# Head work paced by an account of every operation and transfer, loads recorded a step ahead, and q^T S of the samples as fp32 products with a masked q

## The chip, the cores and the metric

The kernel runs on one core of a Trainium2 chip. The metric is the device time of one execution in microseconds (us). TensorE (PE) multiplies, VectorE (DVE) and ScalarE (ACT) do elementwise work, GpSimd (POOL) does small elementwise work and issues transfers, SyncE (SP) issues transfers only. Each engine takes its instructions in the order in which they were recorded.

## The reference

One inference step of a one-layer recurrent decoder on a prompt of 512 tokens and on 8 samples of one token each, 520 columns in all. One projection of x (2048 wide) feeds three mixers: A has 8 heads of 128, B and C have 4 heads of 256. Then come the branch projections, weighted by sigmoid gates, the output projection and a LayerNorm. Cut to what the change touches:

```python
    (hq, hf, hi, hz, rq, rk, rv, rz, mq, mk, mv, mz, mo, mi, mf, gates) = jnp.split(x @ w_in, SPLIT_POINTS, axis=-1)
    ...
    def step(s, inp):                      # mixer A, one chunk of the sequence
        qc, kc, vc, gc = inp
        bc = jnp.cumsum(gc, axis=1)
        o = jnp.einsum('bthk,bhkv->bthv', qc * jnp.exp(bc), s)
        ...
        s_new = jnp.exp(last)[..., None] * s + jnp.einsum('bshk,bshv->bhkv', k_dec, vc)
    ...
    branch = jnp.einsum('blnc,ncd->blnd', ys, w_br)
    merged = jnp.sum(jax.nn.sigmoid(gates.reshape(bsz, seq_len, N_BRANCH, D_MODEL)) * branch, axis=2)
    out = merged @ w_o
```

For a sample a head has a state S of its own (128 x 128 in A, 256 x 256 in B and C). It is decayed, gets k v^T added, is written back, and the head's output is q^T S.

## The kernel before

**Dense work.** Every large product runs as two TensorE products in a rounded fp32 type: a weight tile w is split into `hi` (ACT writes it) and `lo` = w - hi (DVE writes it), and hi goes against both parts of x, lo against the upper one. The program is a list of items. An item is 24 or 48 matmuls of 260 columns on one split of 1024 columns. `w_in` is done in 76 units of 256 columns: 2 classical ones, then 74 by Strassen's scheme with 7 items each, whose sums of weight blocks DVE forms in the ring tiles `R` (three of 1 MB) or a DMA forms in `TT` (a second load that accumulates). Then follow 24 branch units and 8 output units. In all this makes 16,656 dense matmuls, `PD<-...` in the profile. Items share three buffers `hi`, two buffers `lo` and four PSUM banks `PD`.

Results of the projection are parked in DRAM (`pk_Af`, `pk_rv`, ...). Gates (`pk_g`) and partial sums (`pk_part`) come back in the branch units, where DVE multiplies them with the banks (L1542, L1546, `bfin`).

**Side work.** The heads run beside the dense items, as Python generators in three queues: preparation, prompt heads (`a_head`, `b_head`, `c_head`) and samples (`a_samp`, `bc_samp`). The dense generator yields every six matmuls, and then `side_step` may let each queue record its next step. Twelve slots `SL` of 520 columns hold what the heads load and compute; `room` and `ssl` share them out. Four more serve the dense work.

**What sets the order.** Nothing is scheduled by a compiler: what is recorded first stands first on its engine. When the next step of a queue is recorded, a small account decides (`Clock`, `TICK`): it adds up estimated TensorE time, and DVE and ACT time on top of it, without operands and without transfers. A step that yields d is due again d x 0.72 us of accounted TensorE time later; `yield 7` after a load is the whole provision for its landing. A step whose operands are late makes its engine wait, and all recorded behind it on this engine waits too.

`dense` records `lo` of the next item, the loads of weights and `hi` of the item after next at the start of an item:

```python
            if i + 1 < len(items):
                items[i + 1].lo()
            it.run("pre")
            for n in nxt.get(i, ()):
                loads[n]()
            if i + 2 < len(items):
                items[i + 2].hi()
```

The q^T S of a sample is formed in `a_samp` and `bc_samp` by scaling the rows of S with q (ACT, DVE), splitting the result with `hilo` (`qsh` by ACT, `qsl` by DVE) and multiplying both with a column of a unit matrix (`e8`) that puts the sum over the rows into the sample's row of one PSUM tile `os`.

Lines: L80 stands for all operations of TensorE, DVE and ACT, since one helper records them; L381 loads weights, L469 and L470 load `TT`, L654 loads parked tiles, L1136 and L1141 load a sample's state and its v (`vs`).

Of the kernel before, what the change touches and what calls it, by code (L numbers as in the profile page):

```python
# [39 lines left out]
class Clock:  # L40

    def __init__(self):
        self.pe = self.dve = self.act = 0.0

    def add(self, eng, us):
        if eng == "pe":
            self.pe += us
        else:
            setattr(self, eng, max(getattr(self, eng), self.pe) + us)


class Counted:
# [3 lines left out]
    def __getattr__(self, op):  # L56
        f = getattr(self._e, op)
        if op in ("dma_start", "preload_act_table_set"):
            return f

        def g(*a, **kw):
            out = kw.get("out", a[0] if a else None)
            big = out
            if op in ("tensor_reduce", "bn_stats"):
                big = kw["in_"]
            n = 1
            for s in big.shape[1:]:
                n *= s
            if self._n == "pe":
                if op == "transpose":  # L70
                    c = 0.109
# [3 lines left out]
            elif self._n == "dve":  # L75
                c = (n + 65) / 960.0
            else:
                c = 0.1 + 0.00085 * n
            self._c.add(self._n, c)
            return f(*a, **kw)  # L80
        return g


TICK = 0.72
# [4 lines left out]
def tile_hybrid_step(  # L89
# [16 lines left out]
    G, SY = nc.gpsimd, nc.sync  # L106
# [51 lines left out]
    held = {"scan": 0, "samp": 0}  # L158

    def sl(who="scan"):  # L160
        t = free["h"].popleft()
# [5 lines left out]
    def ssl():  # L167

        while not spare():
# [3 lines left out]
    def spare(n=1):  # L173
        return len(free["h"]) - n >= max(0, scan_need[0] - held["scan"])

    scan_need = [SCANMAX]

    def room(n):

        scan_need[0] = n  # L180
        while len(free["h"]) < n - held["scan"]:
            yield 1

    def dsl():
        n = 0
        while not free["d"]:
            n += 1
# [10 lines left out]

    def ps():
        return pss.tile([128, 512], F32, tag="s", name="s")  # L200

    def po1():
        return pso.tile([128, 512], F32, tag="os", name="os")
# [22 lines left out]
    e8 = const.tile([128, 8, 8], F32R, name="e8")  # L226
# [35 lines left out]
    class Side:  # L262
# [8 lines left out]
        def step(self):  # L271
# [15 lines left out]
    SLD, SLA = 2.0, 2.0  # L287

    def side_step(force=False):
        for q in (prepq, scanq, sampq):  # L290
            if force or (q.due <= clk.pe and clk.dve - clk.pe <= SLD and clk.act - clk.pe <= SLA):
# [26 lines left out]
    class Item:  # L318

        def __init__(self, src, mm, post=None, keep=None, nosplit=False):  # L320
            self.src, self.mm, self.post, self.hooks = src, mm, post, {}
            self.n = len(items)
            self.keep, self.nosplit = keep, nosplit
            items.append(self)
# [58 lines left out]
    def strassen_unit(col, deint, fin):  # L383
# [11 lines left out]
        def prod(xn, bank, start, stop):  # L395
            xa, xb = X(xn, 0), X(xn, 1)

            def mm(it):
# [7 lines left out]
                for i, (w, x) in enumerate(seq):  # L406
                    T.matmul(o, w, x, start=start and i == 0, stop=i == 23, skip_group_check=not start)
                    if i % 6 == 5 and i < 23:
                        yield
# [55 lines left out]

        if prev and not deint:
# [3 lines left out]
            before.hook(3, lambda: G.dma_start(out=TT, in_=blk(1), accum_op=ADD))  # L470
# [3 lines left out]
        if prev:  # L474
            prev["P4"]()
# [129 lines left out]
    def dense():  # L605
# [7 lines left out]
        for i, it in enumerate(items):  # L613
            it.run("first")
            if i + 1 < len(items):
# [8 lines left out]
            for _ in it.mm(it):  # L624
                yield
                k += 1
                it.run(k)
# [24 lines left out]
    def ld(nm, k):  # L652
        s = sl()
        SY.dma_start(out=v3(s[:, 0:S], 2), in_=d2(ptile(f"{nm}{k}"))[:, :, 0:256])  # L654
# [23 lines left out]
    def hilo(t):  # L678
        hh = small.tile([128, 256], F32R, tag="qsh", name="qsh", bufs=1)
# [1289 lines left out]
```

## Time and profile before

| | us |
|---|---|
| median of 3 runs (2508.32 to 2512.08) | 2510.2 |
| the profiled execution's own time | 2511.26 |
| its span, first to last instruction | 2509.5 |
| TensorE busy | 2318.8 |
| VectorE busy | 1658.9 |
| ScalarE busy | 1102.3 |
| mean granted TensorE clock | 0.969 |

TensorE is the busiest engine. A busy TensorE is not one at its full pace: matmuls overlap, so the pace is read from the starts of rows that follow each other. Where a group's line names a releaser, this is what ended the engine's idle time before it. In the timeline a row merges equal instructions that follow each other. An fp32 product of TensorE stands in the trace as two records (72 products of 256 columns in the program are 144 records), one in the rounded type as one. From 0 to 190 us the kernel starts up, from 190 to 430 heads hardly take part, from 430 to 1230 the heads of A and B and from 1230 to 1975 those of C and most samples run beside the projection; the branch units reach to 2278 and the output units to the end.

### The profile page before, as it was taken

How to read it: one execution, taken by the hardware profiler on the slowest of the kernel's cores; microseconds unless marked ns; L12 is line 12 of the kernel's file. 1: busy time of each engine (PE TensorE's matmuls, PEld its weight loads, DVE VectorE, ACT ScalarE, POOL GpSimd, SP SyncE). 2: the span in 40 equal slices, each digit the busy share in tenths (PEclk: the TensorE clock that was granted, in tenths of full speed). 3: DMA queues.
4: the chain of work that ended last, by engine and by line, in shares of the span. 5: the costliest groups of instructions: out<-in, count | busy, mean ns of one | idle time of the engine just before them, and what ended most of it. 6: DMA issues, size and time to landing. Idle time of an engine off the chain costs nothing.

```text
span 2509.5 us, 45478 instructions
## 1 busy us (share of the span) xinstructions
PE 2318.8 (92%) x18525; PEld 2265.9 (90%) x18525; DVE 1658.9 (66%) x2648; ACT 1102.3 (44%) x1834; POOL 483.7 (19%) x654
## 2 busy tenths in 40 slices
PE   6999999999998999989889999999989999899995
PEld 6899999999998899989789899898989999899995
DVE  4877777787776767777567676777667444453336
ACT  4444444455544444545455555555546321222222
POOL 1032221223221221212122121221222000001002
PEclk9999999999998999999899999999999999999998
DMA  5376665556555565756567787888878657745221
GB/s 169 93 176 190 173 171 166 154 173 178 162 168 158 160 189 177 235 167 190 147 206 203 202 239 203 209 209 228 219 189 225 190 201 240 266 146 177 80 85 68
DMA packets 406769, 450.30 MB, mean 179 GB/s; under 512 B 17024, under 2 KB 358944, under 8 KB 405024
## 3 DMA queue, kind: packets, MB, share of 16 engines
q1 hardware_dynamic: 314992, 313.43, 39.6%
q0 software_dynamic: 91424, 133.90, 22.5%
q8 instruction: 145, 2.38, 0.4%
q14 instruction: 64, 0.52, 0.1%
q10 hardware_dynamic: 144, 0.07, 0.0%
HBM read 364.03 MB, written 83.28 MB: 178 GB/s over the span
## 4 chain that ended last, share of the span: by engine, by line
PE 35%; DMA 11%; DVE 7%; ACT 2%; issue 2%; SPq 1%; POOL 0%; DVEq 0%; ACTq 0%; POOLq 0%
PE PD L80 31%; DMA R<-in_w_in_dram 4%; PE s L80 3%; DMA SL<-pk_g 3%; DVE SL L80 2%; DVE lo L80 2%; DVE R L80 1%; ACT hi L80 1%; DMA SL<-pk_mv 1%; DMA SL<-pk_mo 1%; PE os L80 1%; DMA SL<-pk_mk 1%; DMA TT<-in_w_in_dram 1%; DMA SL<-vs 0%; DMA R<-in_w_branch_dram 0%
## 5 line engine op out<-in xcount | busy, mean ns | idle before, releaser
L80 PE MATMUL PD<-XZ,hi 128*128 128x260 f32 x9888 | 1443.6, 288 | 49.9 <-ACT hi L80 21.2
L80 PEld LDWEIGHTS PD<-XZ,hi 128*128 128x128 f32 x9888 | 1301.4, 192 | 60.7 <-ACT hi L80 24.5
L80 ACT ACTIVATE hi<-R 128x1024 fp32r<-128x1024 f32 (+1 forms) x539 | 566.6, 1058 | 691.3 <-PE PD L80 264.9
L80 DVE TENSOR_TENSOR lo<-R,hi 128x1024 fp32r<-128x1024 f32 (+1 forms) x538 | 646.7, 1204 | 286.2 <-PE PD L80 110.5
L80 PE MATMUL PD<-XZ,lo 128*128 128x260 f32 x4928 | 806.0, 287 | 12.4 <-DVE lo L80 12.4
L80 PEld LDWEIGHTS PD<-XZ,lo 128*128 128x128 f32 x4928 | 685.9, 191 | 14.7 <-DVE lo L80 14.1
L80 ACT ACTIVATE SL<-PD 128x260 f32<-128x260 f32 x304 | 114.5, 378 | 244.5 <-PE PD L80 164.0
L80 DVE TENSOR_TENSOR R<-R,R 128x1024 f32<-128x1024 f32 x148 | 180.3, 1218 | 14.5 <-DMA R<-in_w_in_dram 14.5
L646 POOL COPY smp<-SL 128x8 f32<-128x8 f32 x104 | 77.0, 740 | 546.9 <-ACT SL L80 322.5
L80 PE MATMUL s<-SL 128*128 128x64 f32 (+5 forms) x976 | 168.0, 311 | 13.9 <-ACT SL L80 7.2
L80 DVE TENSOR_TENSOR SL<-PD,SL 128x260 f32<-128x260 f32 x222 | 94.4, 425 | 126.6 <-PE PD L80 93.3
L80 DVE TENSOR_TENSOR SL<-SL 128x256 f32<-128x256 f32 (+9 forms) x315 | 146.6, 502 | 41.9 <-PE s L80 20.5
L80 PE MATMUL PD<-X,hi 128*128 128x260 f32 x1184 | 159.0, 285 | 0.0
L80 PEld LDWEIGHTS s<-SL 128*128 128x128 f32 (+1 forms) x976 | 139.3, 193 | 21.4 <-ACT SL L80 7.8
L470 POOL DMA_DIRECT2D TT<-in_w_in_dram x57 | 91.4, 1604 | 347.5 <-DMA TT<-in_w_in_dram 300.4
L80 PEld LDWEIGHTS PD<-X,hi 128*128 128x128 f32 x1184 | 149.3, 190 | 0.5
L80 ACT ACTIVATE SL<-SL 128x512 f32<-128x512 f32 (+5 forms) x160 | 88.3, 567 | 60.2 <-DVE SL L80 50.7
L637 POOL TENSOR_TENSOR rstd<-rva,half 128x4 f32<-128x4 f32 (+3 forms) x35 | 52.0, 1485 | 319.8 <-DVE rva L80 318.9
L80 PE MATMUL s<-ident,SL 128*128 128x128 f32 x389 | 68.1, 295 | 46.1 <-DMA SL<-pk_rv 16.0
L80 PEld LDWEIGHTS s<-ident,SL 128*128 128x128 f32 x389 | 49.4, 150 | 52.2 <-issue 26.7
L80 DVE TENSOR_TENSOR SL<-SL,PD 128x260 f32<-128x260 f32 x96 | 36.5, 422 | 88.9 <-DMA SL<-pk_g 58.4
L80 DVE TENSOR_TENSOR lo<-TT,hi 128x1024 fp32r<-128x1024 f32 x74 | 90.0, 1217 | 3.2 <-ACT hi L80 3.2
(221 smaller groups left out, 1610.1 us busy)
## 6 DMA issues: line engine op xcount, KB each, us to landing
R<-in_w_in_dram SPq DMA_DIRECT2D x150, 1024.0 KB, 6.1
TT<-in_w_in_dram SPq DMA_DIRECT2D x57, 512.0 KB, 6.3
TT<-in_w_in_dram POOLq DMA_DIRECT2D x57, 512.0 KB, 6.3
R<-in_w_branch_dram SPq DMA_DIRECT2D x24, 1024.0 KB, 5.7
out_dram<-SL POOLq DMA_DIRECT2D x88, 256.0 KB, 5.7
R<-in_w_out_dram SPq DMA_DIRECT2D x16, 1024.0 KB, 5.7
pk_g<-SL POOLq DMA_DIRECT2D x48, 260.0 KB, 4.6
SL<-pk_g SPq DMA_DIRECT2D x48, 260.0 KB, 6.0
```

What stands on the lines that cost most here:

```text
L80: return f(*a, **kw)
L470: before.hook(3, lambda: G.dma_start(out=TT, in_=blk(1), accum_op=ADD))
L637: G.tensor_tensor(out=r[0:p, 0:n], in0=a[0:p, 0:n], in1=half[0:p, 0:n], op=ALU.pow)
L646: G.tensor_copy(d2(sm(nm, k)), d2(o)[:, :, 256:HN])
```

## The change

1. **The account.** `Clock` keeps a time for each engine, POOL and SP included, the time at which each slot, tile or piece of `XZ` was last written and read, and one pipe for transfers. An operation starts when its engine and its operands are ready. `Side.step` makes the next step due 0.2 us after the latest operation or awaited transfer of this one (and 0.3 us of TensorE time later at the earliest); the number after `yield` no longer counts. Loads marked `pre=True` are not awaited there; instead `late(...)` keeps a head stepping idly until the account has them landed. fp32 products are charged 0.00085 us a column, half of before.
2. **Loads a step ahead.** In A the next head's f and q are loaded during this head, v and z together; in B k with q, in C q and k with v; z before the norm; in the branch units gates and partial sums are asked for one unit earlier, into a head's slot if need be.
3. **Dense order.** `dense` yields every three matmuls. The weight loads and `hi` of the item after next are recorded after 12 matmuls of an item instead of at its start, the first item of a Strassen unit (`late`) gets hi at the start of the item before it and lo after 12 matmuls, and the accumulating load of `TT` is issued 18 matmuls later.
4. **q^T S.** `qmask` multiplies q with the unit matrix into `qmt` (128 x 8 x 8, one column of q in its own row), and TensorE multiplies its slices with S itself in fp32. The scaling of S by q, `hilo` and their 96 + 96 operations are gone. In B and C the update of S is recorded in two halves of 256 columns instead of one of 512, the second in place of v.

```diff
+    def op(self, eng, cost, outs, ins):
+        t = self.t[eng]
...
+        for k in ki:
+            t = max(t, self.after(self.w, k, eng))
+        for k in ko:
+            t = max(t, self.after(self.w, k, eng), self.after(self.r, k, eng))
+        self.t[eng] = e = t + cost
...
+        self.pipe = max(self.pipe, t) + n / (300e3 if n > 4e5 else 230e3)
+        end = max(self.pipe, t) + (3.0 if accum else 2.0)
...
-                    c = max(0.06, 0.00046 * n) if a[2].dtype == F32R else 2 * max(0.06, 0.00085 * n)
+                    t = max(0.06, 0.00046 * n) if a[2].dtype == F32R else max(0.06, 0.00085 * n)
...
-TICK = 0.72
+TICK = 0.3
...
-                    d = next(self.q[0][1])
-
-                    self.due = max(clk.pe + (d or 1) * TICK, clk.dve + 0.5, clk.act + 0.5)
+                    clk.latest = 0.0
+                    next(self.q[0][1])
+
+                    self.due = max(clk.pe + TICK, clk.latest + 0.2)
...
+    def late(*ts):
+        return not forced[0] and clk.ready(*ts) > clk.pe + 0.5
...
-            if force or (q.due <= clk.pe and clk.dve - clk.pe <= SLD and clk.act - clk.pe <= SLA):
+            if force or (q.due <= clk.pe and clk.dve <= clk.next + SLD and clk.act <= clk.next + SLA):
...
+            clk.next = clk.pe + 2.87
+            if i + 1 < len(items) and not items[i + 1].late:
                 items[i + 1].lo()
             it.run("pre")
-            for n in nxt.get(i, ()):
-                loads[n]()
-            if i + 2 < len(items):
-                items[i + 2].hi()
+            if i + 1 < len(items) and items[i + 1].late:
+                items[i + 1].hi()
...
+                if k == 2:
+                    for n in nxt.get(i, ()):
+                        loads[n]()
+                    if i + 1 < len(items) and items[i + 1].late:
+                        items[i + 1].lo()
+                    if i + 2 < len(items) and not items[i + 2].late:
+                        items[i + 2].hi()
...
+    def qmask(q, e):
+
+        t = qmt[:, e]
+        V.tensor_tensor(out=t, in0=e8, in1=q.unsqueeze(2).to_broadcast([128, NS, 8]), op=MUL)
+        return t
...
+        if h < 7 and f"Af{h + 1}" in done and f"Aq{h + 1}" in done:
+            ahead[h + 1] = ld("Af", h + 1, True), ld("Aq", h + 1, True)
...
                 for b in bs:
                     st = lds.pop(b)
-                    V.scalar_tensor_tensor(out=tm[b][:, 0:256], in0=st[:, 256:512], scalar=q[1][:, b:b + 1],
-                                           in1=tm[b][:, 0:256], op0=MUL, op1=ADD)
+                    for e in range(2):
+                        T.matmul(po[0:NS, 0:256], qm[e][:, b, :], st[:, e * 256:(e + 1) * 256],
+                                 start=(b == 0 and e == 0), stop=(b == 7 and e == 1))
                     fr(st)
                 yield 1
-                for b in bs:
-                    hh, ll = yield from hilo(tm[b][:, 0:256])
-                    fr(tm[b])
-                    yield 1
-                    T.matmul(po[0:NS, 0:256], e8[:, b, :], hh, start=(b == 0), stop=False)
-                    T.matmul(po[0:NS, 0:256], e8[:, b, :], ll, start=False, stop=(b == 7))
...
         v = [ld("mv", 2 * h), ld("mv", 2 * h + 1)]
-        yield 7
+        q = [ld("mq", 2 * h + e, True) for e in range(2)]
+        k = [ld("mk", 2 * h + e, True) for e in range(2)]
+        yield 1
...
         for t in range(2):
-            items[k + t].hook(1, sigload(n, 2 * i + t))
+            if (n, i) != (0, 0):
+                items[k - 2 + t].hook(2, sigload(n, 2 * i + t, False))
+            items[k + t].hook(1, sigload(n, 2 * i + t, True))
```

How far a load is ahead of its reader can be counted in the recorded program: the dense matmuls recorded between the load (SP or POOL) and the first instruction that reads its slot, median over the loads of a kind.

| load | before | after |
|---|---|---|
| `pk_rv` (B, v) | 42 | 87 |
| `pk_mv` (C, v) | 45 | 100 |
| `pk_mk` (C, k) | 48 | 229 |
| `pk_mo` (C, output gate) | 48 | 73 |
| `pk_Af` (A, f) | 54 | 99 |
| `vs` (samples, v) | 42 | 84 |
| `pk_g` (branch gates) | 54 | 132 |
| `R` from `in_w_in` | 48 | 60 |

The same count from `hi` to the first product that reads it is 48 before in 519 items; after, it is 36 in 445 items and 24 in 73. From `lo` it is 40 in 517 items before; after, 40 in 444 and 28 in 74.

The first place is SP at the start of a head of C. `pk_mv`, `pk_mq` and `pk_mk` are the parked v, q and k, `R` and `TT` are dense weights. Before:

```order
L654 DMA SL<-pk_mv_9666 128x2x256
L381 DMA R_115<-in_w_in_dram 128x8x256
L1136 DMA SL<-in_state_ret_dram 128x512
L381 DMA R_116<-in_w_in_dram 128x8x256
L469 DMA TT<-in_w_in_dram 128x8x128
L654 DMA SL<-pk_mq_8995 128x2x256
L654 DMA SL<-pk_mq_9089 128x2x256
L654 DMA SL<-pk_mk_9255 128x2x256
L654 DMA SL<-pk_mk_9386 128x2x256
```

After:

```order
L142 DMA SL<-pk_mv_9380 128x2x256
L142 DMA SL<-pk_mq_8729 128x2x256
L142 DMA SL<-pk_mq_8883 128x2x256
L142 DMA SL<-pk_mk_9047 128x2x256
L142 DMA SL<-pk_mk_9158 128x2x256
L142 DMA TT<-in_w_in_dram 128x8x128
L142 DMA R_118<-in_w_in_dram 128x8x256
```

The four loads of q and k moved ahead of three weight loads, behind v.

The second place is TensorE at the first samples of B, between dense items. `os` is the PSUM tile of the samples, `s` that of the prompt heads, `ident` the unit matrix of a transpose. Before:

```order
L80 MATMUL PD_125<-XZ,hi_121 128x260 x16
L80 MATMUL PD_125<-XZ,lo_123 128x260 x2
L80 MATMUL s<-ident,SL 128x128 x4
L80 MATMUL PD_125<-XZ,lo_123 128x260 x6
L80 MATMUL os<-qsh,e_91 8x256
L80 MATMUL os<-qsl,e_91 8x256
L80 MATMUL PD_124<-XZ,hi_119 128x260 x6
```

After:

```order
L165 MATMUL PD_127<-XZ,lo_123 128x260 x5
L165 MATMUL s<-SL,AT 128x256
L165 MATMUL s<-SL 128x256 x4
L165 MATMUL PD_127<-XZ,lo_123 128x260 x3
L165 MATMUL os<-SL,qmt 8x256 x4
L165 MATMUL PD_126<-XZ,hi_121 128x260 x16
```

Two samples now have four products in one row, read from the state itself; a side step can stand between three dense matmuls.

The third place is SP in the last branch units, at the gates of unit 5 (`pk_g_10`, `pk_g_11`) and their partial sums. Before:

```order
L381 DMA R_117<-in_w_out_dram 128x8x256
L1542 DMA SL<-pk_g_10_19610 128x520
L1546 DMA SL<-pk_part_20707 128x520
L1542 DMA SL<-pk_g_11_19707 128x520
L1546 DMA SL<-pk_part_20735 128x520
L381 DMA R_115<-in_w_out_dram 128x8x256
```

After:

```order
L142 DMA R_117<-in_w_branch_dram 128x8x256
L142 DMA SL<-pk_g_10_19100 128x520
L142 DMA SL<-pk_part_20158 128x520
L142 DMA SL<-pk_g_11_19187 128x520
L142 DMA SL<-pk_part_20186 128x520
L142 DMA R_118<-in_w_out_dram 128x8x256
```

The pair stood between the first two loads of output weights and now stands ahead of the first: one unit earlier.

More of the change, by code (lines that the diff above doesn't have):

```diff
@@ L40 @@
 class Clock:
+    LAT = 0.12
     def __init__(self):
[L43 to L49, printed above, removed]
+        self.t = dict(pe=0.0, dve=0.0, act=0.0, pool=0.0, sp=0.0)
+        self.pipe = 0.0
+        self.w, self.r = {}, {}
+        self.alias = {}
+        self.latest = 0.0
+        self.side = False
+        self.next = 0.0
+    pe = property(lambda self: self.t["pe"])
@@ new lines, with keys @@
+    dve = property(lambda self: self.t["dve"])
+    act = property(lambda self: self.t["act"])
+    def keys(self, ap):
+        nm = ap.name
+        nm = self.alias.get(nm, nm)
+        if nm.startswith(("in_", "out_", "c_")):
+            return []
+        cut = CHUNK.get(nm.split("_")[0])
+        if cut is None:
+            return [nm]
+        ext = sum(abs(st) * (n - 1) for st, n in list(ap.ap)[1:])
+        return [(nm, i) for i in range(ap.offset % SPAN[nm.split("_")[0]] // cut,
+                                       (ap.offset % SPAN[nm.split("_")[0]] + ext) // cut + 1)]
@@ L167, in ssl @@
     def ssl():
-        while not spare():
+        while not (spare() or (asked[0] and held["samp"] and len(free["h"]) > max(0, scan_need[0] - held["scan"]))):
             yield 1
@@ L474, in strassen_unit @@
         if prev:
+            one.late = True
+            for f in added:
+                one.hook(2, f)
             prev["P4"]()
@@ L809, in a_head @@
         fr(K, f)
-        yield from room(6)
-        yield 4
+        yield from wait(f"Av{h}", f"Az{h}")
+        v, z = ld("Av", h, True), ld("Az", h, True)
+        yield 1
         level(2, 4)
@@ L816, in a_head @@
         level(8, 2)
-        yield from wait(f"Av{h}")
-        v = ld("Av", h)
-        yield 8
+        yield 1
+        while late(v):
+            yield 1
         pv = ps()
@@ L856, in a_head @@
         G.dma_start(out=hg_p[0, 0, h], in_=St[:, 384:512])
-        yield from wait(f"Az{h}")
-        z = ld("Az", h)
-        yield 4
+        yield 1
         po = ps()
@@ L909, in a_samp @@
                 yield from get(4)
+            while late(st, vb):
+                yield 1
             for j in range(4):
@@ L985, in vtok_of, with y_out @@
         return out
-    def y_out(h, br, obs, zn):
-        z = [ld(zn, 2 * h + hv) for hv in range(2)]
-        yield 6
+    def y_out(h, br, obs, z):
+        while late(*z):
+            yield 1
         for hv in range(2):
@@ L1156, in bc_samp @@
                 V.tensor_tensor(out=kn[:, :, e], in0=nt[:, :, e], in1=q[e], op=MUL)
+        qm = [qmask(q[e], e) for e in range(2)]
         po = po1()
         for b0 in range(0, NS, 2):
-            fresh = False
-            for w, f in ((("v", b0), ldv), (b0, lds_)):
-                if w not in lds:
-                    yield from f(b0)
-                    fresh = True
-            if b0 + 1 not in lds and spare(3):
-                yield from lds_(b0 + 1)
-                fresh = True
-            if fresh:
-                yield 6
@@ L1438, in c_head @@
         so = [ld("mo", 2 * h + hv) for hv in range(2)]
-        yield 7
+        z = [ld("mz", 2 * h + hv, True) for hv in range(2)]
+        yield 1
         obs = []
@@ L1450, in c_head @@
         yield 1
-        yield from y_out(h, 2, [o for o, _ in obs], "mz")
+        yield from y_out(h, 2, [o for o, _ in obs], z)
         fr(*ob2)
```

265 lines of the change are left out of this document (164 added, 101 removed).

## The prediction

> **What bounds the kernel now.** I read the page first, then busy time by stage, then TensorE's waits, then the timeline at single waits.
>
> The page's busy line and its clock in 40 slices:
>
> ```profile
> PE 2318.8 (92%) x18525; PEld 2265.9 (90%) x18525; DVE 1658.9 (66%) x2648; ACT 1102.3 (44%) x1834; POOL 483.7 (19%) x654
> PEclk9999999999998999999899999999999999999998
> ```
>
> TensorE sets the time, so two things count: the TensorE work that the change adds, and the time in which TensorE waits or runs at a lower granted clock. The view by stage (width, then busy time and instructions of each engine, granted clock, DMA share, GB/s) shows where these are:
>
> ```profile
> 190.00:430.00 240.00, 240.00 (x2022) 239.21 (x2021) 181.18 (x276) 110.43 (x171) 47.12 (x60) 1.00 0.63 169
> 430.00:1230.00 800.00, 747.76 (x5966) 730.08 (x5964) 591.73 (x957) 396.48 (x706) 191.97 (x254) 0.97 0.61 176
> 1230.00:1975.00 745.00, 686.97 (x5394) 666.59 (x5395) 522.86 (x817) 392.32 (x654) 160.42 (x216) 0.96 0.77 208
> 2140.00:2278.00 138.00, 122.00 (x957) 120.05 (x956) 64.74 (x96) 32.74 (x40) 4.29 (x8) 0.94 0.59 203
> ```
>
> From 190 to 430 us TensorE never idles. Beside the heads it idles 52.2 and 58.0 us, in the last branch units 16.0: 126.2 us that better order could win. The clock costs 0.03 x 800 + 0.04 x 745 + 0.06 x 138 = 62 us more there. TensorE's waits by releaser (sum, times, longest):
>
> ```profile
> PE PD L80 <- ACT hi L80: 21.2, 13, 4.5
> PE PD L80 <- DVE SL L80: 17.3, 7, 9.0
> PE s L80 <- DMA SL<-pk_rv: 16.0, 8, 5.6
> PE PD L80 <- DVE lo L80: 13.9, 10, 4.3
> PE s L80 <- DMA SL<-pk_mo: 11.7, 1, 11.7
> PE os L80 <- DVE qsl L80: 11.0, 16, 1.6
> PE s L80 <- DMA SL<-pk_mv: 7.8, 4, 3.6
> PE os L80 <- ACT qsh L80: 7.5, 7, 2.3
> PE s L80 <- DMA SL<-pk_mk: 6.7, 2, 3.4
> ```
>
> Four kinds: heads that wait for parked tiles (42.2 us), banks that wait for gates in the branch units (17.3), samples that wait for their split (18.5) and dense items that wait for theirs (35.1).
>
> **Part 1: q^T S as fp32 products.** The pace of an fp32 product is read from a head's five products of 256 columns (ten records):
>
> ```profile
> 1108.93 2.32 PE L80 MATMUL s<-SL 128*128 128x256 f32 x10
> 1110.90 0.83 PE L80 MATMUL PD<-XZ,hi 128*128 128x260 f32 x4
> 1111.57 1.12 PE L80 MATMUL PD<-XZ,lo 128*128 128x260 f32 x8
> ```
>
> The five and the four dense ones behind them took 1111.57 - 1108.93 = 2.64 us. A dense matmul in the full stage starts 0.119 us after the one before (240 us hold 2022 of all kinds), which leaves 2.16 / 5 = 0.43 us a product; for 128 columns I take half, 0.215. Old products stand one behind the other here:
>
> ```profile
> 1717.00 0.28 PE L80 MATMUL os<-qsh,e 128*8 128x256 f32 x1
> 1717.11 0.28 PE L80 MATMUL os<-qsl,e 128*8 128x256 f32 x1
> 1717.23 2.07 PE L80 MATMUL PD<-X,hi 128*128 128x260 f32 x16
> ```
>
> That is 0.115 us each, half of it, 0.06, with 128 columns. The program had 128 of each width; now it has 128 of 256 and 64 of 128 columns. New: 128 x 0.43 + 64 x 0.215 = 68.8 us; old: 128 x 0.115 + 128 x 0.06 = 22.4. **+46.4 us**, on the path in full, since TensorE has nothing to hide it behind: it is the bound. (Bounds: +41 with 0.39 a product, as the first two starts alone give; +47.)
>
> For it the 18.5 us of waits for `qsh` and `qsl` lose their cause. In their place the product waits for DVE's update of S; the step is due when the account has this done, and DVE has 66% to do. I leave 4: **-14.5** (none to -18.5). The work taken off ACT and DVE was hidden behind TensorE, so by itself it gives nothing.
>
> **Part 2: loads ahead.** The transfers (KB, us from issue to landing) and the one long wait as the chain of waits has it (start, length):
>
> ```profile
> R<-in_w_in_dram SPq DMA_DIRECT2D x150, 1024.0 KB, 6.1
> SL<-pk_g SPq DMA_DIRECT2D x48, 260.0 KB, 6.0
> SL<-pk_rv SPq DMA_DIRECT2D x8, 256.0 KB, 7.3
> SL<-pk_mo SPq DMA_DIRECT2D x8, 256.0 KB, 6.2
> 1221.68 15.48 DMA SL<-pk_mo
> ```
>
> Leads are counted in dense matmuls of 0.119 us. v of B had 42, 5.0 us, against 7.3 to land; there are as many waits as loads. It now has 87, 10.4 us. v and k of C go from 45 and 48 to 100 and 229. `pk_mo` goes from 48 to 73, 8.7 us: enough for the median, not for the one of 15.5. I leave 6 of 42.2: **-36** (-20 to -42). The next user of SP is a weight load behind four parked ones; that is the second rival.
>
> In the branch units the lead was about 54, 6.4 us, against 6.0, and failed whenever a transfer was slow:
>
> ```profile
> 2183.01 0.76 DVE L80 TENSOR_TENSOR SL<-SL,PD 128x260 f32<-128x260 f32 x2 [12.83 <-DMA SL<-pk_g]
> 2183.58 1.26 PE L80 MATMUL PD<-XZ,hi 128*128 128x260 f32 x4 [8.99 <-DVE SL L80]
> ```
>
> DVE waited for a gate, the bank stayed full, TensorE stood. With 132, 15.7 us, even the 12.83 is covered: **-16** (-10 to -17).
>
> **Part 3: dense order and account.** Two effects oppose. `hi` is recorded 36 matmuls ahead instead of 48, so 1.4 us of cover goes. On the other side ACT stands less behind transfers that are not there:
>
> ```profile
> ACT SL L80 <- DMA SL<-vs: 39.5, 12, 6.4
> ACT hi L80 <- DMA R<-in_w_in_dram: 155.7, 64, 10.2
> ```
>
> The first is the samples' v, whose lead doubles (42 to 84). The second is ACT waiting for weights two items before they are used; the first item of a unit now asks 24 matmuls ahead instead of 48, when they have had 60 to land instead of 48. What ACT then does meanwhile for heads is no longer late. I take a fifth of 35.1 and a little: **-8** (-25 to the third rival).
>
> At the start of the Strassen units the recorded order has 20 sums and differences of 520 columns on DVE between the last classical item and the first Strassen split, where before there were 9, because the new account starts the preparation later; TensorE covers 4 more gate products.
>
> ```profile
> 93.62 0.70 DVE L80 TENSOR_TENSOR SL<-SL 128x520 f32<-128x520 f32 x1
> 96.92 2.10 PE L80 MATMUL PD<-XZ,lo 128*128 128x260 f32 x8 [4.01 <-DVE lo L80]
> ```
>
> Eleven more at 0.70 us, less 0.5 for the gates: this wait grows by **+7** (0 to +9).
>
> **The clock.** A long wait is paid twice:
>
> ```profile
> 888.16 0.30 PE L80 MATMUL s<-ident,SL 128*128 128x128 f32 x1 [2.63 <-DMA SL<-pk_rv]
> ...
> 889.96 0.88 PE L80 MATMUL PD<-XZ,hi 128*128 128x260 f32 x6
> 890.67 0.60 PE L80 MATMUL s<-ident,SL 128*128 128x128 f32 x4
> ...
> 1091.63 0.45 PE L80 MATMUL s<-ident,SL 128*128 128x128 f32 x1 [5.65 <-DMA SL<-pk_rv]
> ...
> 1093.00 2.86 PE L80 MATMUL PD<-XZ,hi 128*128 128x260 f32 x12
> 1095.70 0.60 PE L80 MATMUL s<-ident,SL 128*128 128x128 f32 x4
> ```
>
> After 5.65 us idle twelve matmuls took 2.70 us, 0.225 each; after 2.63 us idle six took 0.71, 0.118 each. The waits that I remove (36 + 16 + 14.5 + 8 = 74.5 of 126.2) would carry 0.59 x 62 = 37 us of clock in proportion, but many are short: **-24** (-11 to -37).
>
> [...]
>
> **Sum.** 46.4 - 14.5 - 36 - 16 - 8 + 7 - 24 = -45.1 us. The profiled span of 2509.5 becomes 2464.4; its own time was 1.8 above its span: **2466 us**. That execution is 1.1 above the median of the runs, inside their spread.
>
> **Rivals.**
>
> *The account wins more* (0.26). If operands and transfers in the account remove most side waits, 100 of the 126.2 us idle and 45 of the 62 of clock come back: 2509.5 + 46.4 + 7 - 145 + 1.8 = 2420. For it: 190 to 430 us shows that the dense work itself never waits. Against: transfers of 15.48 us stay unforeseen.
>
> *Weights pay for the loads* (0.12). At each head of C four parked loads move ahead of three weight loads, 1 MB at 208 GB/s, 5 us; ACT already waits for weights 64 times, so they have little to spare, and the DMA share there is 0.77. Then 36 us come back as waits for `hi`, the splits gain nothing, and of the clock 8 are left: 2509.5 + 46.4 - 14.5 - 16 + 7 - 8 + 1.8 = 2526, slower. It decides once TensorE's waits for `hi` grow by about 46 us, 0.3 us for each of the 150 weight loads. Against: SP sends each transfer 10 us or more before its user, and the bytes stay the same.
>
> [...]
>
> *Splits come too late* (0.06). Some 410 items stand beside side work (1545 us hold 11360 instructions, some 10,000 of them dense, 24 an item). If one in eight waits 1.6 us (21.2 / 13), that is 82 us: 2548. ACT's 44% speaks against.
>
> *The parts cancel* (0.06): with 0.55 of each gain 54 of the 98.5 us come in against 53.4 of cost, 2510.
>
> **Chances and range.** The forecast has 0.50, with 2440 to 2492 of its own from the bounds. Less than 0.2%, 5 us, can hardly be told from no change here. Faster 0.76, same 0.06, slower 0.18. For 8 in 10 the range runs from below the first rival, 2415, to short of the second, 2520.
>
> **What would show it.** Right: no wait of `s` for `pk_rv`, `pk_mk`, `pk_mv` above 2 us in all; no DVE wait for `pk_g` beyond 20 us in all; `os<-SL,qmt` of 256 columns at 0.43 us; the clock from 430 to 1975 at 0.98. Wrong: waits for `hi` and `lo` above 70 us, or `os` waiting for DVE's update of S more than 15 us in all, or a granted clock as before.

## The result

The changed kernel takes 2397.4 us (median; 2391.0 to 2402.5) against 2510.7 of the kernel before beside it: a ratio of 0.955 with a 95% interval of 0.952 to 0.957. The forecast was 2466 and its range began at 2415, so the change did better than the whole range. Of the cases named, the first rival ("the account wins more", 2420) is nearest. The profiled execution has a span of 2396.3 us, 113.2 less than before.

### The profile page after: what moved, and what is told of

Its sections match the earlier page's. It is cut to its first block, busy times and chain, and to the rows that moved or that the text cites. A ratio compares the mean times of both kernels' runs of the same rounds, so it can differ in the third digit from the quotient of the medians.

```text
span 2396.3 us, 45401 instructions
## 1 busy us (share of the span) xinstructions
PE 2322.9 (97%) x18653; PEld 2242.9 (94%) x18653; DVE 1610.6 (67%) x2576; ACT 1036.0 (43%) x1610; POOL 490.8 (20%) x654
## 4 chain that ended last, share of the span: by engine, by line
PE 86%; DMA 5%; DVE 2%; issue 1%; ACT 1%; POOL 0%; SPq 0%; ACTq 0%; POOLq 0%; DVEq 0%
PE PD L165 75%; PE s L165 8%; PE os L165 3%; DMA R<-in_w_in_dram 3%; DMA out_dram<-SL 1%; DVE SL L165 1%; ACT hi L165 1%; DMA TT<-in_w_in_dram 1%; DMA R<-in_w_branch_dram 0%; DVE lo L165 0%; DVE R L165 0%; ACT SL L165 0%; POOL TT L143 0%; ACT TT L165 0%; POOL out_dram L142 0%
## 5 line engine op out<-in xcount | busy, mean ns | idle before, releaser
L165 PE MATMUL PD<-XZ,hi 128*128 128x260 f32 x9888 | 1425.6, 285 | 18.4 <-ACT hi L165 15.4
L165 PEld LDWEIGHTS PD<-XZ,hi 128*128 128x128 f32 x9888 | 1280.2, 189 | 38.0 <-ACT hi L165 18.5
L165 PE MATMUL PD<-XZ,lo 128*128 128x260 f32 x4928 | 795.9, 284 | 8.8 <-DVE lo L165 8.8
L165 POOL COPY smp<-SL 128x8 f32<-128x8 f32 x104 | 103.6, 996 | 517.4 <-ACT SL L165 306.1
L165 PE MATMUL s<-SL 128*128 128x64 f32 (+5 forms) x912 | 147.3, 298 | 0.0
L165 PEld LDWEIGHTS s<-SL 128*128 128x128 f32 (+1 forms) x912 | 125.0, 187 | 6.2
L142 POOL DMA_DIRECT2D out_dram<-SL x100 | 61.1, 616 | 265.3 <-DVE SL L165 253.5
L165 DVE TENSOR_TENSOR R<-R 128x1024 f32<-128x1024 f32 x74 | 90.0, 1217 | 0.0
L165 POOL TENSOR_TENSOR rstd<-rva,half 128x4 f32<-128x4 f32 (+3 forms) x35 | 34.1, 975 | 260.0 <-DVE rva L165 260.0
L165 PE MATMUL PD<-X,lo 128*128 128x260 f32 x592 | 86.1, 284 | 0.0
```

Of the source, the lines that this page charges most:

```text
L142: return f(out=out, in_=in_)
```

## The profile after

The page's busy line and its clock in 40 slices, of the changed kernel:

```profile
PE 2322.9 (97%) x18653; PEld 2242.9 (94%) x18653; DVE 1610.6 (67%) x2576; ACT 1036.0 (43%) x1610; POOL 490.8 (20%) x654
PEclk9999999999999999999999999999999999999997
```

TensorE is idle for 2396.3 - 2322.9 = 73.4 us where it was 190.7. Busy time by stage of the changed kernel (columns as before):

```profile
430.00:1230.00 800.00, 794.00 (x6346) 759.90 (x6345) 604.05 (x964) 384.70 (x621) 210.61 (x276) 1.00 0.65 192
1230.00:1975.00 745.00, 735.78 (x5800) 699.44 (x5799) 494.70 (x791) 357.80 (x537) 150.26 (x208) 1.00 0.79 211
1975.00:2140.00 165.00, 165.00 (x1384) 165.00 (x1383) 86.92 (x131) 42.70 (x49) 9.88 (x19) 1.00 0.70 236
2140.00:2278.00 138.00, 136.57 (x1136) 135.44 (x1134) 53.91 (x95) 32.55 (x45) 11.97 (x24) 1.00 0.46 155
```

Beside the heads the idle time fell from 110.2 to 15.2 us, and the granted clock is 1.00 in both stages (0.97 and 0.96 before). TensorE's waits by releaser (sum, times, longest), all above 3.4 us in sum, and behind them ACT's wait for weights:

```profile
PE PD L165 <- ACT hi L165: 15.6, 14, 4.3
PE s L165 <- DVE smv L165: 11.5, 1, 11.5
PE PD L165 <- DVE lo L165: 8.8, 1, 8.8
PE s L165 <- DMA SL<-in_x_prompt_dram: 3.5, 5, 2.1
```

```profile
ACT hi L165 <- DMA R<-in_w_in_dram: 66.9, 38, 6.7
```

No parked tile, no gate and no split of a sample is left in the list. The one wait for `lo` is at the first Strassen split; the one for `smv` is in the tail.

## Experiments

All are set beside the kernel before. It took 2513.6 us beside x1 to x4, 2509.4 beside x5 to x8, 2514.4 beside x9 to x12 and 2512.5 beside x13 and x14, so a difference between runs of two of these groups is sure to some 5 us only.

### x1: the products alone, in the kernel before

```diff
+                    for e in range(2):
+                        T.matmul(po[0:NS, 0:256], qm[e][:, b, :], st[:, e * 256:(e + 1) * 256],
+                                 start=(b == 0 and e == 0), stop=(b == 7 and e == 1))
...
-                    T.matmul(po[0:NS, 0:256], e8[:, b, :], hh, start=(b == 0), stop=False)
-                    T.matmul(po[0:NS, 0:256], e8[:, b, :], ll, start=False, stop=(b == 7))
```

> The kernel before with q^T S of the samples as fp32 products with a masked q, and nothing else of the change. If pacing and leads did the work (theory 1), the products alone cost their TensorE time, +46.4 us, and save little more than the 18.5 us of waits for the split and some clock, 5 to 10: 2510.7 + 46.4 - 18.5 - 8 = about 2531 us, slower than before. If the missing chain of scaling and splitting on ACT and DVE did it (rival: it is what made the side steps late from 1230 to 1975 us), the 58 us idle and 30 us of clock there go as well: 2510.7 + 46.4 - 88 = about 2469 us, faster than before. TensorE's waits for parked tiles (42 us) stay by theory 1.

Measured: 2552.8 us, ratio 1.016 (1.014 to 1.017). That is 39 us slower than before: theory 1 has the direction, but expected 20. By itself this part loses. The waits for the split are gone, yet TensorE idles as long as before (188.0 us, 190.7 before), since others grew, above all this one (11.7 us before):

```profile
PE s L80 <- DMA SL<-pk_mo: 38.4, 8, 13.0
```

### x2: the change with the split for q^T S

```diff
+        act(out=hh, in_=t, func=AF.Copy)
+        yield 1
+        V.tensor_tensor(out=ll, in0=t, in1=hh.bitcast(F32), op=SUB)
...
-                        T.matmul(po[0:NS, 0:256], qm[e][:, b, :], st[:, e * 256:(e + 1) * 256],
+                    T.matmul(po[0:NS, 0:256], e8[:, b, :], hh, start=(b == 0), stop=False)
+                    T.matmul(po[0:NS, 0:256], e8[:, b, :], ll, start=False, stop=(b == 7))
```

> The changed kernel with q^T S as before: S scaled by q, split into hi and lo, two products in the rounded type. Everything else of the change stays. By theory 1 the account finds places for the longer chain too: TensorE gets 46 us of work back, waits for qsh and qsl stay under 8 us in all, granted clock 0.98 or more: 2397 - 46 + 10 = about 2361 us, faster than the change. By the rival (the missing chain did it) the waits of 18.5 us and clock of some 25 come back and the time is 2397 us or above.

Measured: 2438.5 us, ratio 0.970 (0.968 to 0.972). With 46 us less work for TensorE it is 41 us slower than the change, in the range of the rival. Two rows of this kernel say where (a wait, and a stage):

```profile
PE os L165 <- ACT qsh L165: 53.4, 12, 7.1
```

```profile
1975.00:2140.00 165.00, 94.25 (x653) 78.07 (x653) 88.09 (x196) 58.22 (x113) 28.67 (x50) 0.71 0.65 198
```

Most of the loss stands in one place. Before the branch loads the y of mixer C, every head and sample of C must be recorded; what is left by then is recorded step after step with no dense work between. In the recorded program 66 matmuls of the side work stand together there; in the changed kernel the last sample is done long before. The split's steps are longer chains, so in this account the samples come too late. The run does not price the split itself; x6 does.

### x3: the change with the old dense order

```diff
-            one.late = True
...
-            if i + 1 < len(items) and not items[i + 1].late:
-                items[i + 1].lo()
+            if i + 1 < len(items):
+                items[i + 1].lo()
             it.run("pre")
...
+            for n in nxt.get(i, ()):
+                loads[n]()
+            if i + 2 < len(items):
+                items[i + 2].hi()
...
```

> The changed kernel with the dense order of before: weight loads, hi of the item after next and lo of the next at the start of an item, the first item of a Strassen unit as all others, the accumulating load of TT where it was. Theory 1 (pacing and leads of the side work): ACT again stands longer behind weights that have not landed, so waits of TensorE for hi rise from 15.6 to 25 us and the time to about 2412 us (between 2397 and 2425). Rival (the dense order is what freed ACT and so the side work): TensorE's idle time from 430 to 1975 us rises from 15 to over 60 us and the time to 2450 us or more.

Measured: 2476.9 us, ratio 0.986 (0.984 to 0.987): 79.5 us of the 113 are gone. The time is the rival's, but from 430 to 1975 us TensorE idles 31.6 us, not over 60. Part of the loss is again the last moment for C, with 114 side matmuls together. The stage row of this kernel, then ACT's waits for weights:

```profile
1975.00:2140.00 165.00, 123.32 (x785) 102.41 (x784) 76.85 (x202) 44.00 (x72) 25.66 (x46) 0.84 0.59 183
```

```profile
ACT hi L165 <- DMA R<-in_w_in_dram: 197.0, 74, 9.2
```

### x4: an account that ignores operands

```diff
-        t = self.t[eng]
+        t = max(self.t[eng], self.t["pe"])
...
-        for k in ki:
-            t = max(t, self.after(self.w, k, eng))
-        for k in ko:
-            t = max(t, self.after(self.w, k, eng), self.after(self.r, k, eng))
```

> The changed kernel with an account that does not look at operands: an operation starts at its engine's time, or at TensorE's if this is later, as before the change; landings of transfers are still awaited and loads stay ahead. If tracking operands is what removed the side waits (theory 1), most of the 117 us idle and 54 us of clock beside heads come back where steps wait for each other: 2450 to 2480 us. If leads alone did it (theory 2), the time stays within 15 us, up to 2412 us, and waits for parked tiles stay at zero either way.

Measured: 2401.6 us, ratio 0.955 (0.953 to 0.957): no different from the change. In sum the operands of DVE, ACT and TensorE in the account bring nothing that can be measured; what is left of the account is the time of each engine and the awaited transfers. At the start the operands do count: in the first 190 us TensorE is busy for 153.7 us here and 164.6 in the change. In this account the side work keeps clear of the last moment for C, so it serves as a base below.

### x5: the old dense order in the account without operands

The edits of x3 and x4 together.

> The old dense order again, as in the run before, but with the account that ignores operands. Theory 1 (lost by the account, not by the order): with operands counted, late splits push ACT's time in the account past the gate, side steps are held back, and 114 of their products stood together at the load of branch 2; with operands ignored none is forced there, so 2395 to 2420 us, the stretch 1975 to 2140 full again. Rival (the order itself: splits that ask for weights two items ahead block ACT): ACT's waits for weights stay near 197 us and the time at 2455 or more.

Measured: 2443.6 us, ratio 0.974 (0.972 to 0.975), between the two theories. Of the 79.5 us of x3, 33 came from the last moment for C (2476.9 - 2443.6); 42 are the order's own (2443.6 - 2401.6). Set against the kernel before beside each run, the two are 29 and 46. ACT's waits for weights are 155.5 us here and 56.8 in x4.

### x6: the split in the account without operands

The edits of x2 and x4 together.

> q^T S by the split in two rounded halves again, with the account that ignores operands, so that no side work is left for the load of branch 2. Set beside the same account with fp32 products (2401.6). Theory 1 (the fp32 products cost TensorE 46 us, and waits for the split are small once steps come in time): 2352 to 2372. Rival (waits for qsh and qsl take the gain, as 53 us did in the earlier run): 2395 or more.

Measured: 2384.1 us, ratio 0.950 (0.948 to 0.951), between the two theories; it beats both kernels. So in this program the fp32 products cost 17.5 us against the split by the medians (2401.6 - 2384.1), 13 set against the kernel before beside each run, not 46. The two stages beside the heads, first of x4 (fp32 products), then of x6 (split):

```profile
430.00:1230.00 800.00, 795.61 (x6345) 757.58 (x6344) 615.44 (x1011) 386.28 (x633) 214.25 (x282) 1.00 0.66 195
1230.00:1975.00 745.00, 733.13 (x5802) 701.39 (x5801) 492.99 (x772) 357.55 (x534) 147.04 (x203) 1.00 0.79 209
```

```profile
430.00:1230.00 800.00, 785.28 (x6437) 770.01 (x6437) 643.88 (x1066) 433.54 (x770) 211.16 (x277) 1.00 0.66 194
1230.00:1975.00 745.00, 715.97 (x5769) 703.11 (x5769) 525.22 (x870) 393.92 (x630) 157.33 (x211) 0.99 0.80 218
```

With the split TensorE idles 43.7 instead of 16.3 us there. The 46.4 us of saved work less 27.5 of new idle time is 19, close to the measured difference. ACT and DVE have 84 and 61 us more to do in the two stages.

### x7: gates and partial sums of the branch units at their old place

```diff
-            if (n, i) != (0, 0):
-                items[k - 2 + t].hook(2, sigload(n, 2 * i + t, False))
```

> The change without the earlier gates and partial sums of the branch units; all else stays. Theory 1 (the prediction's term of 16 with its clock): the stretch 2140 to 2278 waits for gates again, 2412 to 2425. Rival (the gates came late because other transfers were in the way, which the new order of weights cures by itself): 2405 or less, DVE's waits for pk_g below 20 us.

Measured: 2409.4 us, ratio 0.961 (0.959 to 0.962), 12 us slower than the change and between both expectations. DVE waits for a gate once, not 14 times and 58.4 us as before the change:

```profile
DVE SL L165 <- DMA SL<-pk_g: 10.3, 1, 10.3
```

So the old place still fails for a slow transfer, but most of the old waits do not come back with it.

### x8: the heads' loads at their old steps, but awaited

```diff
-        q = [ld("mq", 2 * h + e, True) for e in range(2)]
-        k = [ld("mk", 2 * h + e, True) for e in range(2)]
         yield 1
         vt = yield from vtok_of(v, 260)
         fr(*v)
+        q = [ld("mq", 2 * h + e) for e in range(2)]
+        k = [ld("mk", 2 * h + e) for e in range(2)]
```

and the same for f, q, v and z of A, k and z of B, z of C.

> The change with the heads' loads back at their old steps, but a head still steps on only when the account has them landed (leads counted in dense matmuls: v of B 84, q and k of C 124, z 118 and less). Theory 1 (what counts is that the account awaits a landing, not that the load stands a step earlier): 2395 to 2408, no wait for a parked tile above 3 us. Rival (the earlier place of the loads is needed, as the prediction's term of 36 has it): heads take longer, work stands exposed at the end or waits for parked tiles return, 2420 or more.

Measured: 2398.1 us, ratio 0.955 (0.954 to 0.957): the same as the change. The leads still are long (84 dense matmuls for v of B, 124 for q and k of C) because a head steps on only when the account has its loads landed. The earlier place of the loads is worth nothing measurable here; the awaiting makes the lead. TensorE's wait for `hi` in this kernel, 15.6 us in the change:

```profile
PE PD L165 <- ACT hi L165: 10.5, 5, 4.3
```

### x9: an account that takes each transfer as landed when issued

```diff
-        end = max(self.pipe, t) + (3.0 if accum else 2.0)
+        end = t
```

> The change, but in the account every transfer has landed when it is issued; the loads stand at their new, earlier steps. Leads in dense matmuls: v of B 28, v of C 18, output gate of C 12, q and k of C 74, q of B 8, samples' v 22. Theory 1 (the awaited landing is what removes the waits, the earlier place alone does not): waits for parked tiles and for what DVE and ACT make of them come back, 2435 to 2500. Rival (the earlier place does it, since all the operands of an engine are still counted): 2410 or less.

Measured: 2554.1 us, ratio 1.016 (1.014 to 1.019). That is beyond both expectations: the whole gain is gone and 40 us more. The old provision for a landing (the number after `yield`) does not count here either, so this kernel has none. TensorE's waits in this kernel, then one of ACT's:

```profile
PE os L165 <- DVE SL L165: 39.8, 14, 11.0
PE s L165 <- DMA SL<-pk_mo: 30.1, 6, 10.2
...
PE s L165 <- DMA SL<-pk_rv: 13.2, 7, 4.8
PE s L165 <- DMA SL<-pk_mv: 12.5, 5, 7.2
```

```profile
ACT SL L165 <- DMA SL<-vs: 114.6, 24, 10.5
```

The output gate of C is asked for only 12 dense matmuls ahead here, v of C 18. ACT stands 114.6 us before the samples' v (0.6 in the change), and TensorE's samples wait 39.8 us for DVE (3.3 in the change).

### x10 and x11: the dense order in halves

On the base of x4. x10 takes the weight loads and `hi` of the item after next back to the item's start; x11 takes back only the first items of the Strassen units and the accumulating load of `TT`.

```diff
+            for n in nxt.get(i, ()):
+                loads[n]()
+            if i + 2 < len(items) and not items[i + 2].late:
+                items[i + 2].hi()
             it.run(0)
```

```diff
-            added.append(lambda: G.dma_start(out=TT, in_=blk(1), accum_op=ADD))
+            before.hook(3, lambda: G.dma_start(out=TT, in_=blk(1), accum_op=ADD))
...
-            one.late = True
-            for f in added:
-                one.hook(2, f)
```

> With the account that ignores operands (2401.6): only the weight loads and hi of the item after next go back to the start of the item. Theory 1 (of the 42 us that the dense order won, most comes from ACT no longer standing before weights): ACT's waits for weights rise from 57 to above 130, 2425 to 2445. Rival (it comes from the first items of the Strassen units and the TT load): 2398 to 2410.

> With the account that ignores operands (2401.6): only the first items of the Strassen units and the accumulating load of TT go back to the old order; weight loads and hi of the item after next stay at 12 matmuls. Theory 1: 2403 to 2418, ACT's waits for weights below 100. Rival (these items made the waits): 2425 or more.

Measured: x10 2436.7 us, ratio 0.970 (0.967 to 0.973); x11 2440.9, ratio 0.971 (0.969 to 0.974). Each half alone costs 35 and 39 us, nearly the 42 of both: the halves do not add up. ACT's waits for weights, first of x10, then of x11:

```profile
ACT hi L161 <- DMA R<-in_w_in_dram: 79.5, 29, 9.2
```

```profile
ACT hi L161 <- DMA R<-in_w_in_dram: 221.3, 68, 12.6
```

In x10 ACT's waits grow little (56.8 in x4), so the theory got the time and missed the reason. What stands out there is SP: the 150 weight loads leave 1.9 us (median) after TensorE has begun the dense matmul recorded next behind them, against 0.4 in x4 and 0.4 in x11. In x11 SP is in time, ACT stands, and the rival has the time. That the lateness of SP is what costs x10 its 35 us is read from this number; no run tests it.

### x12: the split with fewer steps

x6 with the split's steps joined and the constants of the side work set up with the samples.

```diff
         act(out=hh, in_=t, func=AF.Copy)
-        yield 1
         V.tensor_tensor(out=ll, in0=t, in1=hh.bitcast(F32), op=SUB)
...
-        prepq.append(("const", const_setup()))
+        sampq.append(("const", const_setup()))
```

> q^T S by the split, account without operands (2384.1), and two things more: the split's steps are recorded in fewer pieces, and the constants of the side work are set up with the samples instead of in the preparation, ahead of the first Strassen unit. Theory 1 (the wait of 16 us at the first Strassen split and the longer chains cost what they show): 2362 to 2380, the wait for lo at the start below 10. Rival (the wait moves to the gates behind it): 2380 or more.

Measured: 2401.4 us, ratio 0.955 (0.952 to 0.958). The wait for `lo` at the start, 16.1 us in x6, is gone, but `os` waits for `qsh` 12.4 us instead, and TensorE for `hi` 31.2 instead of 20.9: the rival's case. Which of its two edits lost the 12 to 17 us is not told apart.

### x13 and x14: account and order, each alone, in the kernel before

x13 is the account without operands with the loads ahead, and all else as before (old dense order, split, late gates). x14 is the kernel before with only the new dense order:

```diff
-            if i + 1 < len(items):
+            if i + 1 < len(items) and not items[i + 1].late:
                 items[i + 1].lo()
             it.run("pre")
-            for n in nxt.get(i, ()):
-                loads[n]()
-            if i + 2 < len(items):
-                items[i + 2].hi()
+            if i + 1 < len(items) and items[i + 1].late:
+                items[i + 1].hi()
...
+                if k == 2:
+                    for n in nxt.get(i, ()):
+                        loads[n]()
...
```

> From the other side: account with awaited landings and loads ahead (operands ignored), but the old dense order, the split for q^T S and the late gates, all as in the kernel before. Theory 1 (awaiting landings is worth the largest share by itself, and the parts roughly add up: 2401.6 + 42 for the order + 12 for the gates - 17 for the products): 2430 to 2447. Rival (without the new dense order ACT stands before weights and eats most of it): 2470 or more.

> The kernel before with the new dense order alone (weight loads and hi after 12 matmuls, first items of the Strassen units, TT load). Theory 1 (the 42 us are the order's own, whatever paces the heads): 2462 to 2478, ACT's waits for weights below 90 (156 before). Rival (it pays only where the side work comes in time; the prediction's term of 8): 2495 or more.

Measured: x13 2478.3 us, ratio 0.988 (0.984 to 0.991), 34 us faster than before, as its rival had it; x14 2446.3, ratio 0.974 (0.969 to 0.978), 66 us faster and better than its theory. The order needs no account, and alone it brings more than the account and all the earlier loads. Rows of x14: waits of TensorE, of ACT, of DVE and of SP, then the stage of the last branch units:

```profile
PE PD L80 <- ACT hi L80: 33.7, 15, 4.9
...
PE s L80 <- DMA SL<-pk_mo: 15.0, 5, 9.0
...
PE PD L80 <- DVE SL L80: 10.0, 2, 9.4
...
PE s L80 <- DMA SL<-pk_mv: 6.8, 6, 2.7
...
PE PD L80 <- DVE lo L80: 3.2, 3, 2.5
...
PE s L80 <- DMA SL<-pk_rv: 1.1, 2, 0.6
```

```profile
ACT hi L80 <- DMA R<-in_w_in_dram: 63.9, 25, 9.3
```

```profile
DVE SL L80 <- DMA SL<-pk_g: 11.8, 1, 11.8
```

```profile
SPq L382 <- DVE lo L80: 1140.2, 128, 30.0
```

```profile
2140.00:2278.00 138.00, 136.56 (x1117) 135.43 (x1117) 66.78 (x106) 36.63 (x47) 10.43 (x21) 0.98 0.52 167
```

The same waits of DVE and of SP in the kernel before, then SP's timeline there at one head of B (start, length, transfers issued):

```profile
DVE SL L80 <- DMA SL<-pk_g: 58.4, 14, 12.8
```

```profile
SPq L381 <- DVE lo L80: 1436.7, 136, 30.1
```

```profile
855.56 2.40 SPq L654 DMA_DIRECT2D SL<-pk_rk  x2
879.26 2.85 SPq L381 DMA_DIRECT2D R<-in_w_in_dram  x2
882.20 1.20 SPq L654 DMA_DIRECT2D SL<-pk_rv  x2
```

No parked load and no gate was moved in x14, yet the waits for `pk_rv` fell from 16.0 to 1.1 us, those for `pk_mk` (6.7) are gone, and DVE's for gates fell from 58.4 to 11.8 (TensorE's behind them from 17.3 to 10.0; one long wait is left). The rows of SP tell why. A weight load waits on SP until the last `lo` of its ring tile is done, and all transfers recorded behind it wait on SP too: in the timeline `pk_rv` leaves at 882.20 us, behind two weight loads that SP could issue only from 879.26, and TensorE waits for it 2.63 us (the row at 888.16). With the loads recorded 12 matmuls later SP stands 189 us less before weight loads (1805.5 and 1616.8 us, summed over all releasers, of which the rows show the largest), though only 49 less in all: it now also waits before gates and partial sums. The weight loads then leave 0.5 us (median) after TensorE has begun the dense matmul recorded next behind them instead of 2.4, and gates leave 2.3 us ahead of that point instead of 1.2 behind it.

## Why the prediction was wrong, step by step

By its own terms, the idle time and busy time of the two profiles give this. Idle time fell by 190.7 - 73.4 = 117.3 us; busy time rose by only 4.1, with 46.4 of new work in it, so 42.3 came back from the clock (mean granted clock 0.969 before, 0.990 after). (A second count agrees: dense matmuls of the kernel before start 0.218 us apart at a granted clock of 0.50 and 0.119 at 1.00, medians; half of TensorE's busy time in the stretches at 0.50, an estimate of what 1.00 would have saved, is 52.8 us before and 8.7 after, 44 less.)

| step | forecast | in the two profiles |
|---|---|---|
| fp32 products on TensorE | +46.4 | +46.4 |
| waits for the samples' split and update of S | -14.5 | -20.5 |
| waits for parked tiles | -36 | -42.2 |
| waits for gates | -16 | -16.7 |
| waits for `hi` and `lo`, start included | -8 + 7 | -10.7 |
| other waits | none | -27.2 |
| clock | -24 | -42.3 |
| sum | -45.1 | -113.2 |

**Products: right in price, not in what they are worth.** A record of 256 columns starts 216 ns before the next one, one of 128 columns 109 ns (medians): 256 x 0.216 + 128 x 0.109 = 69.3 us, against 22.9 for the old ones by their medians. But the run without them (x6) gains only 13 to 17.5, because TensorE saves 46.4 us of work and idles 27.5 more beside the heads, where ACT and DVE have the split to do. So "The work taken off ACT and DVE was hidden behind TensorE, so by itself it gives nothing" does not hold in the changed program; in the kernel before it nearly does, where the products cost 39 of their 46.4 (x1).

**Loads and gates: the sums right, the cause half wrong.** The waits went as forecast. But part 2 counted a lead from where a load is recorded, and x14 shows that it counts from where SP gets to it. The new dense order alone takes away nearly all waits for `pk_rv` and `pk_mk` and 7.3 of the 17.3 us behind gates, with none of these loads moved. The waits for `pk_mo` and `pk_mv` need more (15.0 and 6.8 us remain in x14), and x8 with x9 shows that in the new account the awaited landing does it, not the earlier place.

**Part 3 is the step that failed.** "-8" for order and account looked at the waits for `hi` and `lo` alone and took ACT's 155.7 us before weights as hardly worth anything. The order alone is worth 66 us in the kernel before (x14), and 42 to 46 in the new one (x5 against x4). In x14 the waits for `hi` and `lo` together did not fall at all (35.1 and 36.9 us). What fell are the waits for v and k of the heads (`pk_rv`, `pk_mk`: 22.7 to 1.1), those behind gates (17.3 to 10.0), those for ACT's writes to slots (20.9 to 10.4), and with the idle time (39.3 us less) the loss to the clock (22.6 less busy time for the same work, mean granted clock 0.979 against 0.969). So the order acts on other paths than the one that the prediction priced: SP stands less before a ring tile in use, with other transfers behind it, and ACT less before weights in flight (155.7 to 63.9). Most of the 27.2 us of "other waits" stood in the list of before and were left out of the prediction's four kinds: TensorE waiting for ACT's writes to slots.

```profile
PE s L80 <- ACT SL L80: 8.8, 4, 4.2
...
PE PD L80 <- ACT SL L80: 6.6, 4, 2.4
PE os L80 <- ACT SL L80: 5.5, 4, 2.4
```

These 20.9 us of the kernel before are 0.9 in the changed one, where ACT stands less before weights (66.9 us) and the samples' v (0.6 instead of 39.5). That this is the reason is not shown: 12.0 us are left in x13, where ACT stands 196.2 us before weights.

**Clock: a term sized too small.** 42.3 us came back, not 24. The -24 was the author's estimate between two ends; no row or run shows its end of -11. The prediction took one wait of 2.63 us that cost nothing more and one of 5.65 that did, and concluded that only long waits count. The traces show another reason. In both profiles the granted clock is 1.00 or 0.50, and each of its changes falls on a grid of 3.413 us. These are windows of this grid in the kernel before (columns as before, the granted clock behind the five busy times), at the waits of 2.63 us (884 to 891), of 2.98 (986 to 993) and of 5.65 (from 1085):

```profile
884.00:887.41 3.41, 1.54 (x13) 1.33 (x12) 1.60 (x2) 2.36 (x3) 2.21 (x4) 1.00 1.08 345
887.41:890.82 3.41, 2.27 (x18) 2.11 (x19) 0.61 (x2) 0.60 (x1) 0.00 (x0) 1.00 1.09 349
986.39:989.80 3.41, 0.95 (x7) 0.80 (x8) 1.06 (x2) 0.07 (x1) 0.00 (x0) 1.00 0.65 232
989.80:993.21 3.41, 3.41 (x19) 3.25 (x18) 2.32 (x3) 1.57 (x2) 0.00 (x0) 0.50 0.00 0
...
1085.38:1088.80 3.42, 0.61 (x6) 0.40 (x4) 1.07 (x3) 1.90 (x4) 0.94 (x2) 1.00 1.06 335
1088.80:1092.21 3.41, 0.45 (x1) 0.18 (x1) 2.28 (x3) 0.00 (x0) 0.00 (x0) 0.50 1.00 354
1092.21:1095.62 3.41, 3.15 (x15) 3.18 (x16) 0.00 (x0) 1.54 (x2) 0.00 (x0) 0.50 0.01 5
1095.62:1099.04 3.42, 3.42 (x32) 3.37 (x32) 0.43 (x1) 1.74 (x2) 0.00 (x0) 1.00 0.00 0
```

The wait of 2.63 us falls on a border of the grid: the two windows have 1.87 and 1.14 us of idle time, and the clock stayed full. The one of 2.98 lay in one window, 2.46 of it idle, and the next window ran at half. In the kernel before each of the 22 windows at 1.00 with 2.1 us or more idle (the tail left out) had one at 0.50 behind it, so here a removed wait was worth more than its length already from about 2 us on, if it fell into one window; 25 stretches at half rate (133 us, the tail left out) became 4 (20 us).

**The signs.** All signs of being right that the prediction named came true (no wait of `s` for `pk_rv`, `pk_mk` or `pk_mv`, none of DVE for gates, 0.43 us a product of 256 columns, a clock of 1.00 where 0.98 stood), and none of being wrong. They tested parts 1 and 2 and the clock; none of them looked at what the order brings elsewhere.

**The rivals.** "The account wins more" came nearest, but half its reason fell: operands in the account bring nothing in sum (x4), landings do (x9). "Weights pay for the loads" is refuted: TensorE's waits for `hi` fell from 21.2 to 15.6 us and ACT's for weights from 155.7 to 66.9. The dense order helps there too, so x8 is the closer test: without the earlier loads of the heads TensorE waits 5 us less for `hi`, where this rival needed 46. "Splits come too late" did not happen; the longest wait for `hi` is 4.3 us. At the start the wait for `lo` went from 4.0 to 8.8 us, +4.8 where +7 stood.

**What stays open.** The parts do not add up. From the side of the kernel before, order -66, account with loads -34 and products +39 make -61, and the gates' 12 of x7, part of which x14 already has, make it -73; together they gave -113. That the products cost less in the new program (13 to 17.5 against 39) explains 22 to 26 of the 40 missing. Two rows may bear on the rest: in x13 ACT stands 196.2 us before weights, and its account without operands loses time at the start (TensorE busy 150.3 of the first 190 us, 162.6 in the kernel before). How the rest divides was not measured, and no run takes back the yield every three matmuls or the update of S in halves by itself.

## What to carry to other kernels

In this kernel a load's lead began when its queue reached it, not where it was recorded (x14: the waits for `pk_rv` fell from 16.0 to 1.1 us with none of these loads moved): look at what the issuing engine waits for ahead of it, and record a transfer that needs a buffer late enough that the buffer is free. To pace side work, await the modelled landing of its transfers: without any provision for it this kernel lost 157 us (x9), without its operands 4, within the noise (x4). Price a change of order by all the waits behind the queues that it frees, not only by those of the operands that it moves (x14: 66 us, with the waits for `hi` and `lo` at 36.9 us where they were 35.1). Work taken off the bounding engine was worth its time only as far as the engines that took it over stayed in time (x6: 46.4 us of work saved, 27.5 of new idle time, 13 to 17.5 gained).

## What had not been expected of the hardware

In the traces of the kernel before and of the changed one the granted clock changes only on a grid of 3.413 us. Over these two, in windows at a clock of 1.00 (the last 30 us left out), 2.1 us or more of idle TensorE time was followed by 0.50 in 26 of 26 cases, less than 1.2 us in none of 1314, and between them in 3 of 19. From 0.50 it came back after a window with less than 0.6 us idle (29 of 29) and never after one with more (0 of 16).
